# Masked softmax with per-batch lengths: the load of batch 3 is cut in halves that go behind the first two stores, and GpSimd's start is rearranged

## Chip, cores, metric

One core of a Trainium2 chip. The metric is the device time of one execution in microseconds; medians of several executions are given.

## The reference

For each of 16 batches there are 8 heads of 256 x 256 float32. Only the first `length` columns of a row count; the others come out as zero.

```python
for b in range(batch):
    length = lengths[b]                      # 128..255, known only at run time
    masked = x[b, :, :, :length]
    e = np.exp(masked - masked.max(-1, keepdims=True))
    result[b, :, :, :length] = e / e.sum(-1, keepdims=True)   # the rest stays 0
```

## The kernel before

A batch is one slot of a tile with 8 slots: 128 partitions x 16 rows x 256 columns, 2 MB. SyncE loads batches 0 to 3 whole (0 in halves). GpSimd loads 4 to 15, each only as wide as its length needs, into slots whose right part it has filled with zeros. Per batch VectorE masks (`clip`), ScalarE takes the exponential and the row sums, VectorE divides in two halves, and SyncE stores (most batches as a half and two quarters).

```python
        for h in range(2):                                  # load 0 in halves
            s = slice(h * half, (h + 1) * half)
            nc.sync.dma_start(out=xt[:, 0, s], in_=x_f[0, :, s]).then_inc(s_ld[h], 16)
        nc.scalar.dma_start(out=word64, in_=lengths[None, :]).then_inc(s_word, 16)
        for b in range(1, ahead):                           # loads 1, 2, 3; ahead = 4
            nc.sync.dma_start(out=xt[:, b], in_=x_f[b]).then_inc(s_ld[b + 1], 16)
        for b in range(batch):                              # all stores, same queue
            s_b = s_st[b % 2]
            for s in parts(b):
                nc.sync.wait_ge(s_out, 2 * b + (s.stop - 1) // half + 1)
                ...
                nc.sync.dma_start(out=out_f[b, :, s, :], in_=xt[:, b % slots, s, :]
                ).then_inc(s_b, 16 * ((s.stop - s.start) // quarter))
        ...
        # GpSimd
        nc.gpsimd.dma_start(out=word64_p, in_=lengths[None, :]).then_inc(s_word_p, 16)
        ...
        nc.gpsimd.wait_ge(s_v, 1)                           # VectorE's first step
        for b in range(ahead, slots):
            nc.gpsimd.memset(xt[:, b, :, low:], 0.0).then_inc(s_fill, 1)
        nc.gpsimd.wait_ge(s_word_p, 16)
        nc.gpsimd.wait_ge(s_fill, slots - ahead)
        nc.gpsimd.wait_ge(s_ld[ahead - 1], 16)              # load 2 has landed
        # ... then the loads of batches 4 to 15, two in flight
        ...
        # VectorE, start: cast of the lengths, matmul broadcasts them, bounds in step 2
        nc.vector.wait_ge(s_word, 16)
        nc.vector.tensor_copy(out=len_b, in_=word[:, ::2]).then_inc(s_lenb, 1)
        nc.vector.wait_ge(s_lenf, 1)
        step(nc.vector.tensor_scalar(out=len_s, in0=len_f, scalar1=big, ...))   # s_v = 2
```

VectorE's order is mask 0a, mask 0b, divide 0a, mask 1, divide 0b, mask 2, divide 1a, divide 1b, mask 3, and so on (a and b are the halves of a batch). A store waits for its divide. At most two batches of stores are in flight.

The softmax here doesn't subtract the row's maximum and nothing guards it: scores larger than these inputs give would overflow.

## Time and profile before

| | before |
|---|---|
| median time | 157.06 us (3 runs, 156.97 to 157.08) |
| bytes moved | 62.08 MB |
| busiest compute engine | VectorE, 77% |
| both DMA queues, share of the 16 engines' time | 65.9% + 32.0% |
| first store: issued, first packet | 16.73 us, 23.43 us |
| first load of GpSimd: issued, first packet | 20.71 us, 25.71 us |

The last two rows join the timeline with the packet records. The page's DMA row gives the busy tenths of the DMA engines in 40 slices of 3.9 us, and the row below it GB/s. A high digit with low GB/s means that packets are in flight but slow. The lines themselves stand in the prediction.

### The profile page before, as it was taken

The page shows a single profiled execution, that of the slowest core. Times are in us where ns is not written, and L with a number is a line of the kernel's source. Part 1 is how long each engine was busy: PE and PEld are TensorE (multiplying, and loading weights), DVE is VectorE, ACT ScalarE, POOL GpSimd, SP SyncE. Part 2 cuts the span into 40 slices and gives each one's busy share as a digit, 9 for nine tenths or more (in the row PEclk, how much of TensorE's full clock was granted, in tenths as well). Part 3 has the DMA queues.
Part 4 walks back from the last instruction along what each step waited for, and adds up shares of the span by engine and source line. Part 5 has one row for each costly group of instructions (what it writes and reads, how often), then busy time and mean ns, then how long its engine had stood idle before and what let it go on. Part 6 is the DMA issues. An engine that isn't in the chain of part 4 may idle for free.

```text
span 155.5 us, 1320 instructions
## 1 busy us (share of the span) xinstructions
PE 0.2 (0%) x1; PEld 0.1 (0%) x1; DVE 120.0 (77%) x84; ACT 105.1 (68%) x514; POOL 19.4 (12%) x26
## 2 busy tenths in 40 slices
PE   0000000000000000000000000000000000000000
PEld 0000000000000000000000000000000000000000
DVE  4963999999999968939895999997977999920000
ACT  3029599999989893956969298989592989400000
POOL 7900031003020202002020202020100000000000
DMA  4999999999999999999999999999999999999991
GB/s 116 428 443 426 434 312 388 416 442 427 393 395 410 415 416 406 420 410 413 409 412 419 402 417 406 415 411 405 425 421 432 420 419 432 457 426 422 415 434 61
DMA packets 10452, 62.08 MB, mean 399 GB/s; under 512 B 930, under 2 KB 1026, under 8 KB 7122
## 3 DMA queue, kind: packets, MB, share of 16 engines
q1 hardware_dynamic: 6336, 41.95, 65.9%
q0 software_dynamic: 4112, 20.12, 32.0%
q14 instruction: 2, 0.02, 0.0%
q10 hardware_dynamic: 2, 0.00, 0.0%
HBM read 28.51 MB, written 33.55 MB: 399 GB/s over the span
## 4 chain that ended last, share of the span: by engine, by line
DMA 67%; DVE 11%; issue 6%; POOLq 2%; SPq 1%; POOL 0%; DVEq 0%
DMA xt<-in_x_dram 60%; DVE xt L224 7%; DMA out_dram<-xt 7%; DVE xt L197 3%; POOLq L100 1%; POOLq L136 1%; POOLq L131 1%; SPq L109 1%; DVE inv_sum L221 0%; POOL xt L131 0%; SPq L112 0%; POOLq L159 0%; POOLq L155 0%; DVEq L214 0%; POOLq L161 0%
## 5 line engine op out<-in xcount | busy, mean ns | idle before, releaser
L251 ACT ACTIVATE xt<-xt x256 | 102.4, 402 | 27.2 <-DVE xt L197 27.2
L224 DVE TENSOR_TENSOR xt<-xt,inv_sum 128x2048 f32<-128x2048 f32 x32 | 73.3, 2292 | 1.1
L251 ACT ACTIVATION_READ_ACCUMULATOR xt<-xt x256 | 48.2, 188 | 0.0
L197 DVE SCALAR_TENSOR_TENSOR xt<-down,len_s,xt 128x2048 f32<-128x2048 f32 (+1 forms) x17 | 37.7, 2222 | 11.1 <-DMA xt<-in_x_dram 10.2
L131 POOL DMA_DIRECT2D xt<-in_x_dram x12 | 12.7, 1057 | 89.7 <-issue 45.7
L221 DVE RECIPROCAL inv_sum<-row_sum 128x8 f32<-128x8 f32 x32 | 6.2, 195 | 2.4 <-ACT xt L251 2.4
L185 DVE CAST len_b<-word 1x16 bf16<-1x16 int32 x1 | 5.6, 5595 | 0.4 <-DMA word<-in_lengths_dram 0.4
L151 POOL MEMSET xt<- 128x1536 f32 x4 | 5.3, 1392 | 0.0
L243 ACT ACT_TABLE_LOAD x1 | 1.3, 1283 | 1.6 <-SPq L79 1.6
L180 DVE TENSOR_SCALAR down<-iota_i 128x256 f32<-128x256 int32 x1 | 0.3, 295 | 1.6 <-POOL iota_i L142 1.6
L146 POOL DMA_DIRECT2D word_p<-in_lengths_dram x1 | 0.6, 643 | 0.1
L188 DVE TENSOR_SCALAR len_s<-len_f 128x16 f32<-128x16 f32 x1 | 0.2, 174 | 0.4 <-PE len_f L167 0.4
L142 POOL IOTA iota_i<- 128x256 int32 x1 | 0.3, 331 | 0.6 <-SPq L79 0.6
L243 ACT ACTIVATE warm<-const-float32-0.0 128x1 f32<-128x1 f32 x1 | 0.2, 203 | 0.0
L145 POOL MEMSET ones<- 1x128 bf16 x1 | 0.2, 194 | 0.0
L167 PE MATMUL len_f<-len_b,ones 1*128 1x16 bf16 x1 | 0.2, 168 | 8.0 <-DVE len_b L185 8.0
L269 POOL MEMSET const-float32-0.0<- 128x1 f32 x1 | 0.1, 98 | 0.3 <-issue 0.3
L148 POOL MEMSET seed<- 1x1 f32 x2 | 0.1, 88 | 0.0
L167 PEld LDWEIGHTS len_f<-len_b,ones 1*128 1x128 bf16 x1 | 0.1, 98 | 8.0 <-issue 8.0
L269 POOL MEMSET const-float32-1.0<- 128x1 f32 x1 | 0.1, 98 | 0.0
L269 POOL MEMSET const-bfloat16-1.0<- 128x1 bf16 x1 | 0.1, 98 | 0.0
L269 POOL MEMSET const-uint8-127<- 128x1 uint8 x1 | 0.1, 98 | 0.0
(1 smaller groups left out, 0.0 us busy)
## 6 DMA issues: line engine op xcount, KB each, us to landing
out_dram<-xt SPq DMA_DIRECT2D x16, 1024.0 KB
out_dram<-xt SPq DMA_DIRECT2D x20, 512.0 KB
xt<-in_x_dram SPq DMA_DIRECT2D x3, 2048.0 KB, 16.0
out_dram<-xt SPq DMA_DIRECT2D x3, 2048.0 KB
xt<-in_x_dram POOLq DMA_DIRECT2D x3, 1728.0 KB, 15.9
xt<-in_x_dram POOLq DMA_DIRECT2D x2, 2048.0 KB, 16.0
xt<-in_x_dram POOLq DMA_DIRECT2D x2, 1600.0 KB, 14.5
xt<-in_x_dram POOLq DMA_DIRECT2D x2, 1280.0 KB, 13.6
```

What stands on the lines that cost most here:

```text
L100: return nc.values_load(at, engines=[engine], skip_runtime_bounds_check_because="compared with constants, never an address",)
L109: nc.sync.dma_start(out=xt[:, 0, s], in_=x_f[0, :, s]).then_inc(s_ld[h], 16)
L131: nc.gpsimd.dma_start(out=xt[:, slot, :, :w], in_=x_n[:, n, :, :w]).then_inc(s_sw[par], 16)
L136: with nc.gpsimd.If(v <= ws[m]):
L146: nc.gpsimd.dma_start(out=word64_p, in_=lengths[None, :]).then_inc(s_word_p, 16)
L151: nc.gpsimd.memset(xt[:, b, :, low:], 0.0).then_inc(s_fill, 1)
L185: nc.vector.tensor_copy(out=len_b, in_=word[:, ::2]).then_inc(s_lenb, 1)
L197: return nc.vector.scalar_tensor_tensor(out=t, in0=down[:, None, lo:hi].to_broadcast([P, s.stop - s.start, hi - lo]), scalar=len_s[:, b : ...
L221: step(nc.vector.reciprocal(out=inv_sum[:, b, s], in_=row_sum[:, b, s]))
L224: nc.vector.tensor_tensor(out=t, in0=t, in1=inv_sum[:, b, s, None].to_broadcast([P, half, seq_k]), op=ALU.mult,).then_inc(s_out, 1)
L243: nc.scalar.activation(out=warm, in_=nc.const_aps.tensor(0.0, (P, 1), F32), func=EXP)
L251: ins = nc.scalar.activation(out=e, in_=e, func=EXP, accum_out=sum_h[:, bass.ds(i, 1), j])
```

## The change

Two ideas. First, SyncE issues load 3 in halves, one behind store 0a and one behind store 0b, so that the first store need not queue behind all of load 3; store 0b then goes out in one piece instead of two quarters. Second, the fills wait for the bounds (the scaled lengths in every partition, VectorE's second step), so that they don't hold up VectorE's cast of the lengths, and GpSimd reads the lengths that ScalarE fetched.

```diff
         def parts(b):
-        if b < 10:
+        if b == 0:
+            cuts = [0, half, nt]
+        elif b < 10:
             cuts = [0, half, half + quarter, nt]
 ...
-        for b in range(1, ahead):
+        for b in range(1, ahead - 1):
             nc.sync.dma_start(out=xt[:, b], in_=x_f[b]).then_inc(s_ld[b + 1], 16)
+        last = [
+            (s_ld[ahead + h], slice(h * half, (h + 1) * half)) for h in range(2)
+        ]
 ...                                        # behind each store, while halves are left:
+                if last:
+                    s_l, r = last.pop(0)
+                    nc.sync.dma_start(out=xt[:, ahead - 1, r], in_=x_f[ahead - 1, :, r]).then_inc(s_l, 16)
 ...
-        nc.gpsimd.dma_start(out=word64_p, in_=lengths[None, :]).then_inc(s_word_p, 16)
 ...
-        nc.gpsimd.wait_ge(s_v, 1)
+        nc.gpsimd.wait_ge(s_v, 2)
 ...
-        nc.gpsimd.wait_ge(s_word_p, 16)
+        nc.gpsimd.wait_ge(s_word, 16)
 ...                                        # VectorE, mask of batch 3:
+                if b == ahead - 1:
+                    nc.vector.wait_ge(s_ld[b + 2], 16)
```

More of the change, by code (lines that the diff above doesn't have):

```diff
@@ L65 @@
     word = word64.bitcast(I32)
-    word64_p = pool.tile([1, batch], mybir.dt.int64, name="word64_p")
-    word_p = word64_p.bitcast(I32)
     len_b = pool.tile([1, batch], BF16, name="len_b")
@@ L81 @@
         s_word = sem("s_word")
-        s_word_p = sem("s_word_p")
         s_ones = sem("s_ones")
@@ L85 @@
         s_lenf = sem("s_lenf")
-        s_ld = [sem(f"s_ld{k}") for k in range(ahead + 1)]
+        s_ld = [sem(f"s_ld{k}") for k in range(ahead + 2)]
         s_sw = [sem("s_sw0"), sem("s_sw1")]
@@ L104, in length @@
             )
+        nc.scalar.dma_start(out=word64, in_=lengths[None, :]).then_inc(s_word, 16)
         for h in range(2):
@@ L109 @@
             nc.sync.dma_start(out=xt[:, 0, s], in_=x_f[0, :, s]).then_inc(s_ld[h], 16)
-        nc.scalar.dma_start(out=word64, in_=lengths[None, :]).then_inc(s_word, 16)
-        for b in range(1, ahead):
+        for b in range(1, ahead - 1):
             nc.sync.dma_start(out=xt[:, b], in_=x_f[b]).then_inc(s_ld[b + 1], 16)
+        last = [
+            (s_ld[ahead + h], slice(h * half, (h + 1) * half)) for h in range(2)
+        ]
         for b in range(batch):
@@ L157 @@
                 n = 2 * q + (ahead + par)
-                v_len = length(POOL, word_p[0:1, bass.ds(2 * n, 1)])
+                v_len = length(POOL, word[0:1, bass.ds(2 * n, 1)])
                 with nc.gpsimd.If(q >= 1):
```

## The prediction

> **What bounds the kernel now.** I read the page first: engines, slices, queues.
>
> ```profile
> PE 0.2 (0%) x1; PEld 0.1 (0%) x1; DVE 120.0 (77%) x84; ACT 105.1 (68%) x514; POOL 19.4 (12%) x26
> ...
> DMA  4999999999999999999999999999999999999991
> GB/s 116 428 443 426 434 312 388 416 442 427 393 395 410 415 416 406 420 410 413 409 412 419 402 417 406 415 411 405 425 421 432 420 419 432 457 426 422 415 434 61
> ...
> q1 hardware_dynamic: 6336, 41.95, 65.9%
> q0 software_dynamic: 4112, 20.12, 32.0%
> ```
>
> No compute engine is above 77%, while the DMA row is at 9 from the second slice to the last but one. SyncE's queue (q1) and GpSimd's (q0) fill 97.9% of the 16 engines' time. So the bound is bytes through the DMA engines: 62.08 MB. A change can win only where the engines move less than they could. One slice stands out, the sixth with 312. I cut the span finer (columns: stretch, length, busy time of each engine, clock, DMA share, GB/s):
>
> ```profile
> 2.00:3.00 1.00, 0.00 (x0) 0.00 (x0) 0.70 (x1) 0.99 (x2) 1.00 (x4) 1.00 0.93 205
> 3.00:4.00 1.00, 0.00 (x0) 0.00 (x0) 1.00 (x1) 0.14 (x1) 1.00 (x2) 1.00 0.82 287
> ...
> 8.00:20.00 12.00, 0.17 (x1) 0.10 (x1) 8.42 (x8) 7.28 (x36) 0.00 (x0) 1.00 1.01 432
> 20.00:21.00 1.00, 0.00 (x0) 0.00 (x0) 1.00 (x1) 1.00 (x7) 0.28 (x1) 1.00 1.34 426
> 21.00:22.00 1.00, 0.00 (x0) 0.00 (x0) 1.00 (x2) 1.00 (x6) 0.92 (x1) 1.00 1.19 279
> 22.00:23.00 1.00, 0.00 (x0) 0.00 (x0) 1.00 (x1) 1.00 (x7) 0.00 (x0) 1.00 0.57 197
> 23.00:24.00 1.00, 0.00 (x0) 0.00 (x0) 0.97 (x3) 1.00 (x6) 0.51 (x1) 1.00 0.73 270
> 24.00:25.00 1.00, 0.00 (x0) 0.00 (x0) 1.00 (x1) 1.00 (x7) 0.03 (x1) 1.00 0.96 393
> ...
> 41.00:123.00 82.00, 0.00 (x0) 0.00 (x0) 71.09 (x51) 64.99 (x321) 9.77 (x9) 1.00 1.02 413
> 123.00:152.00 29.00, 0.00 (x0) 0.00 (x0) 13.85 (x10) 10.34 (x52) 0.00 (x0) 1.00 1.01 428
> ```
>
> 432 GB/s is what a stretch of whole loads reaches; I take it as the rate to lose against. From 20 to 25 us the loss is 6+153+235+162+39 = 595 KB, or 1.4 us at 432. From the first packet (2.14 us in the packet records) to 4 us some 492 KB moved where 804 could: 0.7 us. From 41 to 123 us 413 stands against 432, 3.6 us in all, but there the software queue moves packets of 1.3 to 4.8 KB, and the change leaves those alone. After the last load (123.7 us) stores alone still run for 30 us at 428: VectorE ends at 137, the last packet at 153.5. Compute has 16 us of slack at the end.
>
> The chain of waits then tells where GpSimd's loads start, and the timeline what VectorE does at the start:
>
> ```profile
> 2.51 16.01 DMA xt<-in_x_dram
> 18.52 0.02 issue
> ```
> ```profile
> 1.83 0.64 POOL L146 DMA_DIRECT2D word_p<-in_lengths_dram  x1
> 2.04 1.90 SPq L112 DMA_DIRECT2D xt<-in_x_dram  x3
> 2.30 5.59 DVE L185 CAST len_b<-word 1x16 bf16<-1x16 int32 x1 [0.40 <-DMA word<-in_lengths_dram]
> 2.47 0.12 POOL L148 MEMSET seed<- 1x1 f32 x2
> 2.54 5.33 POOL L151 MEMSET xt<- 128x1536 f32 x4
> ```
>
> The third whole load (batch 2) lands at 18.52 and opens GpSimd's gate. A cast of 16 numbers takes 5.59 us and ends (7.89) when the four fills do (7.87). Behind it come the matmul, the bounds, and the first mask at 9.29.
>
> **What the Trainium skill says.** "SBUF — State Buffer", section Who interferes with whom: a cast may run in a mode that takes the port pair shared with GpSimd, and then one of the two blocks fully; a VectorE instruction with two SBUF inputs meets GpSimd only where GpSimd reads. The cast agrees (both end within 0.02 us); that the mask (two inputs) runs freely beside a fill (which only writes) no trace here shows yet. "DMA: Bandwidth & Descriptors", section Queues, rings and completion order: an engine alternates between the queues that have work, packet by packet. The packet records agree: from 26 to 32 us q1 moves about 190 GB/s and q0 about 230. Same page, Issuing engines are not separate DMA queues: which engine starts a transfer changes no bandwidth. The 432 of q1 alone against 413 of both agrees that a second queue adds nothing. Same page, Specifications: first byte of the software path about 1 us. The trace disagrees: GpSimd's first x load is issued at 20.71 and its first packet starts at 25.71, and the lengths take 1.83 to about 6.0.
>
> **The change part by part.**
>
> *Fills after the bounds.* The cast starts at 2.30 with no fill running; I give it 0.1 us (estimate: other small VectorE steps took 0.17 to 0.2). Matmul and bounds took 8.01 to 8.42 after the cast, so the bounds stand at about 2.9. The first mask then waits for the first half load, which lands at 6.2 (issue 1.13 plus 5.1, the shorter of the two half loads). Mask from 9.29 to about 6.4: 2.9 us earlier. The second half lands at 8.7, and ScalarE reaches it later. From first mask to first store took 9.29 to 16.73 = 7.44 us, so the first store goes out at 13.8, the second half's at 21.4 - 2.9 = 18.5. The fills move to about 3.0 to 8.4, long before the gate at 18.5. None of these 2.9 us is on the path that sets the end: they only make stores ready.
>
> *Removed lengths load on GpSimd.* 0.64 us of issue and some 4-byte packets. It may have disturbed the first packets (some took 1.0 us instead of 0.31 just after it); at best the 0.7 us of the start. I count 0.2.
>
> *Halves of batch 3 between the stores.* Before, q1 held load 3 from 18.0 to 23.9 and the first store's packets began at 23.4, 6.7 us after issue. Now at 18.0 (end of load 2's packets) q1 finds store 0a, issued at 13.8. At 1.05 MB each and 432 GB/s, 2.43 us: store 0a 18.0 to 20.4, half load 3a to 22.9, store 0b (issued at 18.5, in time) to 25.3, then half load 3b. q0 starts at about 25.7 as before, since its gate is load 2. By then q1 has moved the same bytes in both kernels, only in another order. Load 3b has about 0.9 MB left, which at q1's shared 200 GB/s takes 4.4 us: it lands near 30.5 instead of 24.25. VectorE wants it at 28.46 - 2.9 = 25.6, so a new wait of about 5 us appears in front of the mask of batch 3, and that mask runs some 2 us later than before. Meanwhile q1 has both halves of store 1 (issued at 23.3 and 25.7; 2.1 MB, 10 us at 200 GB/s) and q0 two loads, so the engines do not run dry. No bytes are saved.
>
> Sum: the DMA time stays, except the two weak spots. The start gives 0.2. The 1.4 us at 20 to 25 us: I do not know its cause. Direction changes alone are not it, for at 34 to 38 us loads and stores alternate at 430 GB/s. It begins with GpSimd's first large issue (20.71), which stays; but later issues, as at 36.24, show no dip. I give 35% that it vanishes (-0.5), 50% that it stays, 15% that the three changes of direction in q1 add about 1.3 us (+0.2). 157.06 - 0.2 - 0.5 + 0.2 = 156.6; I say 156.5.
>
> **The rivals.**
>
> *A new wait takes over:* the mask of batch 3 waits for its second half and the delay reaches the end. For: VectorE is in order, and its mask of batch 4 and GpSimd's slots lie behind it. Against: VectorE needs 7.1 us per batch (2.35 + 2 x 2.45) while the DMA delivers one per 9.3 us (3.88 MB at 415), so 2 us are caught up within one or two batches; at the end 16 us are spare. If the queues did run dry for the 2 us: 159.
>
> *The early start is worth its full size:* stores begin 5.4 us sooner and the end moves with them. For: the first store's packets wait 6.7 us behind a load. Against: the engines were busy with that load, which must be done anyway. It would make 152 to 154.
>
> *The dip is load into store within one queue:* now there are two such turns and one back. For: the dip lies exactly on load 3's last three packets per engine (0.65 to 1.38 us instead of 0.61) and ends as the first store packet starts. Against: the mixed stretch without loss. It would make 158 to 158.5.
>
> *The dip goes altogether, and the start is clean:* 155.0.
>
> **Range and chances.** The sure part is zero, the weak spots allow -2.1 and the turns +1.4, with run-to-run spread 0.1. I take 155.3 to 157.7. Faster than 2% needs 153.9, below what both weak spots give; slower than 2% needs 160.2, beyond the dry-queue case. 0.02 and 0.02.
>
> **What would show each step right or wrong.** The cast well under 1 us, the first mask near 6.4 beside the fills at its usual 1.24 us; first store issued near 13.8. Load 3b landing near 30 and a VectorE wait before batch 3's mask. GpSimd's first load still issued near 20.7. In the fine stretches: whether 20 to 25 us stays near 300 GB/s, and the first 2 us. I am wrong if the DMA row falls below 9 between 25 and 45 us (queues dry), if GpSimd's first load comes later because it is now its first transfer, or if the 41 to 123 us rate moves away from 413.

## The result

The changed kernel takes 157.01 us (4 runs, 156.81 to 157.34), the kernel before 157.01 us (4 runs, 156.94 to 157.08). The ratio is 1.0002, 95% interval 0.9984 to 1.002: the same.

The page of the changed kernel, its engines, slices and queues:

```profile
PE 0.2 (0%) x1; PEld 0.1 (0%) x1; DVE 115.2 (74%) x84; ACT 105.3 (68%) x514; POOL 19.0 (12%) x25
...
DMA  4999999999999999999999999999999999999992
GB/s 110 425 438 432 322 423 421 411 411 443 414 404 389 418 406 420 411 408 421 406 416 412 410 421 403 414 409 411 416 409 438 425 423 427 444 432 436 423 413 121
...
q1 hardware_dynamic: 6336, 41.95, 66.1%
q0 software_dynamic: 4080, 20.12, 32.1%
```

The DMA row is as full as before and the bytes are the same. The weak slice has not gone: it was the sixth (312), now it is the fifth (322). The fine stretches of the changed kernel, with columns as in the prediction:

```profile
2.00:3.00 1.00, 0.17 (x1) 0.10 (x1) 0.34 (x2) 0.99 (x2) 0.00 (x0) 1.00 1.02 197
3.00:4.00 1.00, 0.00 (x0) 0.00 (x0) 0.00 (x0) 0.14 (x1) 0.95 (x1) 1.00 0.88 270
9.00:15.00 6.00, 0.00 (x0) 0.00 (x0) 4.82 (x4) 5.56 (x28) 0.00 (x0) 1.00 1.01 431
15.00:16.00 1.00, 0.00 (x0) 0.00 (x0) 1.00 (x1) 0.00 (x0) 0.00 (x0) 1.00 1.21 459
16.00:17.00 1.00, 0.00 (x0) 0.00 (x0) 0.97 (x3) 0.52 (x3) 0.00 (x0) 1.00 1.28 328
17.00:18.00 1.00, 0.00 (x0) 0.00 (x0) 1.00 (x1) 1.00 (x5) 0.00 (x0) 1.00 0.74 246
18.00:19.00 1.00, 0.00 (x0) 0.00 (x0) 0.67 (x1) 1.00 (x7) 0.00 (x0) 1.00 0.62 254
19.00:20.00 1.00, 0.00 (x0) 0.00 (x0) 0.36 (x1) 1.00 (x6) 0.00 (x0) 1.00 1.02 434
20.00:25.00 5.00, 0.00 (x0) 0.00 (x0) 4.93 (x5) 5.00 (x27) 1.59 (x2) 1.00 1.01 423
...
41.00:123.00 82.00, 0.00 (x0) 0.00 (x0) 70.94 (x49) 64.94 (x320) 9.75 (x9) 1.00 1.02 412
123.00:152.00 29.00, 0.00 (x0) 0.00 (x0) 17.09 (x14) 12.99 (x64) 0.00 (x0) 1.00 1.00 427
```

The stretch of slow packets lies from 16 to 19 us, some 5 us earlier than before, and ends where the packets of store 0a begin (18.33 us in the packet records, 23.43 before). By then GpSimd has issued no load at all. From 20 to 25 us, where before was at its worst, the rate is 423. The start (197, 270) is no better than before (205, 287), and the long mixed part is unchanged (412 against 413).

The chain of waits and the timeline of the changed kernel:

```profile
2.51 16.89 DMA xt<-in_x_dram
19.40 0.02 issue
```
```profile
2.30 0.17 DVE L189 CAST len_b<-word 1x16 bf16<-1x16 int32 x1 [0.39 <-DMA word<-in_lengths_dram]
...
3.05 5.33 POOL L155 MEMSET xt<- 128x1536 f32 x4 [1.11 <-DVE len_s L192]
6.51 1.28 DVE L201 SCALAR_TENSOR_TENSOR xt<-down,len_s,xt 128x1024 f32<-128x1024 f32 x1 [3.52 <-DMA xt<-in_x_dram]
...
13.95 0.42 SPq L121 DMA_DIRECT2D out_dram<-xt  x1
14.41 0.36 SPq L126 DMA_DIRECT2D xt<-in_x_dram  x1
...
31.28 2.35 DVE L201 SCALAR_TENSOR_TENSOR xt<-down,len_s,xt 128x2048 f32<-128x2048 f32 x1 [4.41 <-DMA xt<-in_x_dram]
```

The cast takes 0.17 us instead of 5.59. The first mask starts at 6.51 and takes its 1.28 us in the middle of the fills. The first store goes out at 13.95 instead of 16.73. Load 2 is the one that the slow stretch now hits: it lands at 19.40 instead of 18.52, and GpSimd's first load is issued 1.07 us later than before (21.78). The mask of batch 3 waits 4.41 us for the second half of its load. VectorE's gain of 2.9 us at the start has turned into a loss of 2.8 us there (31.28 against 28.46), and still the time is the same.

So two questions are left. What is the slow stretch, and does it cost what it seems? And why does a VectorE that is first earlier and then later not matter: is the whole change idle, or do two effects cancel?

### The profile page after: what moved, and what is told of

Its sections match the earlier page's. It is cut to its first block, busy times and chain, and to the rows that moved or that the text cites. A ratio compares the mean times of both kernels' runs of the same rounds, so it can differ in the third digit from the quotient of the medians.

```text
span 154.9 us, 1320 instructions
## 1 busy us (share of the span) xinstructions
PE 0.2 (0%) x1; PEld 0.1 (0%) x1; DVE 115.2 (74%) x84; ACT 105.3 (68%) x514; POOL 19.0 (12%) x25
## 4 chain that ended last, share of the span: by engine, by line
DMA 71%; DVE 12%; issue 3%; SPq 3%; POOLq 1%; DVEq 0%
DMA out_dram<-xt 40%; DMA xt<-in_x_dram 31%; DVE xt L230 9%; DVE xt L201 3%; SPq L121 2%; SPq L109 1%; DVE inv_sum L227 0%; POOLq L99 0%; SPq L111 0%; POOLq L136 0%; POOLq L141 0%; POOLq L159 0%; DVEq L220 0%; POOLq L163 0%; SPq L120 0%
## 5 line engine op out<-in xcount | busy, mean ns | idle before, releaser
L189 DVE CAST len_b<-word 1x16 bf16<-1x16 int32 x1 | 0.2, 165 | 0.4 <-DMA word<-in_lengths_dram 0.4
```

## The experiments

The theories as the runs were planned. **D:** the DMA engines set the time, so neither part of the change matters. Its rival: the parts have effects that cancel. For the slow stretch, **F:** it is paid once, for the first store of the program; **T:** it is a turn from 16 KB load packets to stores in SyncE's queue; **G:** GpSimd's first large issue causes it (the trace of the changed kernel already speaks against G, since the stretch comes 5 us before that issue). A table of all readings of the slow stretch stands after the runs. The kernel before took a median of 156.91 us beside the first four runs, 156.93 beside the next four, then 156.97 and 157.14.

### fills_only: the second part alone

```diff
 # the kernel before, with:
-        nc.gpsimd.dma_start(out=word64_p, in_=lengths[None, :]).then_inc(s_word_p, 16)
-        nc.gpsimd.wait_ge(s_v, 1)
+        nc.gpsimd.wait_ge(s_v, 2)
-        nc.gpsimd.wait_ge(s_word_p, 16)
+        nc.gpsimd.wait_ge(s_word, 16)
```

> The kernel before with the second part of the change alone (shared lengths, fills after the bounds). My theory (the DMA engines set the time, and an earlier store only waits longer in SyncE's queue): the first store is issued near 13.9 us instead of 16.7, its packets still begin near 23.4 behind load 3, the weak stretch stays at 20 to 24 us (near 280, 200, 270 GB/s), ratio to before 0.998 to 1.002. Rival (the earlier compute start is worth something by itself): ratio below 0.995.

Measured: 157.09 us (6 runs), ratio 1.0012, interval 0.9989 to 1.0036. The first mask is at 6.41 us and the first store is issued at 13.85, as meant. In the fine stretches the weak seconds are where they were in the kernel before:

```profile
21.00:22.00 1.00, 0.00 (x0) 0.00 (x0) 0.96 (x3) 1.00 (x7) 0.98 (x1) 1.00 1.09 246
22.00:23.00 1.00, 0.00 (x0) 0.00 (x0) 1.00 (x1) 1.00 (x6) 0.00 (x0) 1.00 0.63 213
23.00:24.00 1.00, 0.00 (x0) 0.00 (x0) 0.97 (x3) 1.00 (x7) 0.50 (x1) 1.00 0.71 270
```

With the old order an earlier start is worth nothing: the store waits 2.9 us longer behind load 3. It also shows that the slow stretch doesn't follow the time at which the store is issued (13.85 against 16.73); it follows the place of the store in the queue.

### order_only: the first part alone

```diff
 # the changed kernel, with the second part undone:
+        nc.gpsimd.dma_start(out=word64_p, in_=lengths[None, :]).then_inc(s_word_p, 16)
-        nc.gpsimd.wait_ge(s_v, 2)
+        nc.gpsimd.wait_ge(s_v, 1)
-        nc.gpsimd.wait_ge(s_word, 16)
+        nc.gpsimd.wait_ge(s_word_p, 16)
```

> The changed kernel with the second part undone (GpSimd's own lengths load, fills before the bounds). My theory: cast 5.6 us and first store near 16.7 us as before, still ahead of the end of load 2's packets at 18 us, so the queue has no gap; the weak stretch lies at 16 to 18.5 us, before the first store's packets; ratio 0.997 to 1.003. Rival (the order needs the earlier store, else the queue runs dry between load 2 and store 0): ratio above 1.005.

Measured: 158.71 us (6 runs, 158.26 to 159.02), ratio 1.0106, interval 1.008 to 1.0132. My theory missed: the order alone costs some 1.7 us. (This run undoes both halves of the second part, the place of the fills and GpSimd's own load of the lengths; no run tells the two apart.) The reason that the rival gave is not what the trace shows either; store 0a was issued at 16.74, in time for the end of load 2. The loss is elsewhere, and the fine stretches of this kernel and its timeline show it:

```profile
28.00:31.00 3.00, 0.00 (x0) 0.00 (x0) 0.55 (x1) 3.00 (x17) 0.00 (x0) 1.00 0.99 300
31.00:41.00 10.00, 0.00 (x0) 0.00 (x0) 5.93 (x5) 4.50 (x23) 0.49 (x1) 1.00 1.03 431
```
```profile
35.01 2.35 DVE L205 SCALAR_TENSOR_TENSOR xt<-down,len_s,xt 128x2048 f32<-128x2048 f32 x1 [6.45 <-DMA xt<-in_x_dram]
```

From 28 to 31 us the rate is 300 where the changed kernel has 413 in the same stretch: 3 us x (413 - 300) / 432 = 0.8 us lost. The packet records show both queues at loads then (the second half of load 3, and batch 4), with slow packets in both. The engines also drift apart: the second half of load 3 lands on its first engine at 29.1 us and on its last at 34.7 (changed kernel: 29.0 and 31.0). At the very end the last half store lands on fourteen engines by 153.9 us and on the last two at 155.3 and 155.4, where the changed kernel is done at 153.3. So about half of the loss is a slower stretch and the rest two engines that fell behind, by the account of this one profile. It isn't a queue run dry: VectorE is 3.7 us later than in the changed kernel at the mask of batch 3 (35.01 against 31.28), but afterwards the rate is as high (431 from 31 to 41 us against 429, 403 from 41 to 48 us against 399). Why the packets are slow from 28 to 31 us is open. Two kernels below have a weaker dip there (halves_all 369, act_big 376).

### after_warm and before_warm: a tiny early store on ScalarE's queue

```diff
 # the changed kernel, or the kernel before, with:
         nc.scalar.dma_start(out=word64, in_=lengths[None, :]).then_inc(s_word, 16)
+        nc.vector.memset(zero, 0.0).then_inc(s_zero, 1)          # [128, 128] float32
+        nc.scalar.wait_ge(s_zero, 1)
+        nc.scalar.dma_start(out=out_f[0, :, 0, 0:P], in_=zero).then_inc(s_warm, 16)
 ...
+        nc.sync.wait_ge(s_warm, 16)                               # before the first real store
```

> The changed kernel with one tiny early store (128 rows of 512 B of zeros, overwritten later) from ScalarE's queue at about 1.7 us. Theory F (the weak stretch of some 1.2 us is paid once, for the first store of the program, wherever it comes): the stretch at 16 to 18.5 us is gone (above 420 GB/s), time lower by 0.7 to 1.3 us unless it is paid at the start instead, which would show as a worse 2 to 4 us. Theory T (it is the turn from 16 KB load packets to store packets within SyncE's queue): the stretch at 16 to 18.5 us stays near 320, 240, 370 GB/s and the ratio is 1.000 within 0.003.

> The same tiny early store in the kernel before. Theory F: 20 to 24 us rises from 426, 279, 197, 270 to above 400 each, time lower by 0.7 to 1.3 us. Theory T: unchanged there, ratio 1.000 within 0.003. A third (GpSimd's first large issue at 20.7 us does it): unchanged here too, but it has to explain why the changed kernel has the stretch 4 us before that issue.

Measured: after_warm 157.05 us, ratio 1.0004 (0.9982 to 1.0026); before_warm 156.94 us, ratio 1.0007 (0.9981 to 1.0032). The slow stretch stays in both. These 64 KB touch only 512 B of every 8 KB that store 0a writes, so they don't show whether the stretch comes from writing that part of the output for the first time; early_store below does. This looked like T, and it was wrong to read it so, as the next runs show.

### halves_all and whole_between: which packets lie ahead of the store

```diff
 # halves_all: the changed kernel, with
         for b in range(1, ahead - 1):
-            nc.sync.dma_start(out=xt[:, b], in_=x_f[b]).then_inc(s_ld[b + 1], 16)
+            for h in range(2):
+                s = slice(h * half, (h + 1) * half)
+                nc.sync.dma_start(out=xt[:, b, s], in_=x_f[b, :, s]).then_inc(s_ld[b + 1], 16)
 # (waits for loads 1 and 2 raised to 32)
 # whole_between: the changed kernel, with
-        last = [(s_ld[ahead + h], slice(h * half, (h + 1) * half)) for h in range(2)]
+        last = [(s_ld[ahead], slice(0, nt))]          # load 3 whole, behind store 0a
```

> The changed kernel with loads 1 and 2 as halves too, so that the packets ahead of the first store are 8 KB like the store's and not 16 KB. If the weak stretch hangs on the 16 KB load packets, it is gone at 16 to 18.5 us (above 400 GB/s) and the ratio to before is about 0.993. If it belongs to the first store of SyncE's queue whatever the packets, it stays (about 1.2 us lost) and the ratio is 0.998 to 1.003.

> The changed kernel with load 3 whole (16 KB packets) between store 0a and store 0b. If every turn from 16 KB loads to stores costs, there is a second weak stretch near 24 to 26 us, 1.2 us lost more, ratio 1.005 to 1.008. If only the first store costs, no second stretch and 0.998 to 1.003; the landing of load 3 then moves to about 27 us, ahead of 30.97.

Measured: halves_all 156.82 us, ratio 0.9992 (0.9965 to 1.0018); whole_between 157.16 us, ratio 1.0003 (0.9975 to 1.0031). With 8 KB packets ahead the stretch stays. With a second turn from 16 KB loads to stores no second stretch appears (410 GB/s from 22 to 28 us), and load 3 lands at 27.2 us. T falls: neither the size of the load packets ahead of the store nor a later turn matters.

### early_store, tiny_sp, act_big: a store of another size, on another queue, earlier

```diff
 # the changed kernel; zero is [128, 4, 256] float32 = 512 KB, in tiny_sp [128, 128] = 64 KB
 # early_store and tiny_sp, between loads 0 and 1 on SyncE's queue:
+        nc.vector.memset(zero, 0.0).then_inc(s_zero, 1)
+        nc.sync.wait_ge(s_zero, 1)
+        nc.sync.dma_start(out=out_f[batch - 1, :, 0:4, :], in_=zero).then_inc(s_warm, 16)
 # act_big: the same 512 KB with nc.scalar, right behind the lengths
 # all: nc.sync.wait_ge(s_warm, 16) before the first real store
```

> The changed kernel with a 512 KB store of zeros on SyncE's own queue between loads 0 and 1 (512 KB more bytes, 1.2 us at 432 GB/s, overwritten later). If the loss is paid once by the first full-size store of SyncE's queue, it shows near 6 to 9 us and the stretch before store 0a, now near 17 to 20 us, is clean: ratio about 1.008. If the loss belongs to the turn before store 0a whatever went earlier, it stays there, and the ratio is about 1.008 with one stretch or 1.015 with two.

> The changed kernel with a 64 KB store of zeros (128 rows of 512 B) on SyncE's own queue between loads 0 and 1. If what is paid once belongs to the queue that stores for the first time, 15 to 20 us is clean (loss at 432 GB/s below 0.2 us instead of 0.88), and about 1 us is lost near 6 to 9 us instead, or less if a small store pays less; ratio between 0.994 and 1.002. If it belongs to the amount (only a store of some size pays it), 15 to 20 us keeps its 0.9 to 1.1 us and the ratio is 1.001.

> The changed kernel with a 512 KB store of zeros on ScalarE's queue, issued near 1.7 us (1.2 us more of bytes). If the amount decides, SyncE's first store is clean afterwards (15 to 20 us loses below 0.2 us). If the queue decides, the 0.9 to 1.1 us stay there, whatever ScalarE's queue lost before.

Measured: early_store 158.67 us, ratio 1.0108 (1.0076 to 1.014); tiny_sp 156.93 us, ratio 0.9998 (0.9966 to 1.003); act_big 157.66 us, ratio 1.0042 (1.0003 to 1.0081). The fine stretches of early_store:

```profile
5.00:10.00 5.00, 0.00 (x0) 0.00 (x0) 1.51 (x2) 1.87 (x9) 3.45 (x3) 1.00 1.05 372
...
15.00:25.00 10.00, 0.00 (x0) 0.00 (x0) 8.27 (x6) 5.83 (x29) 1.29 (x1) 1.00 1.00 423
```

and of tiny_sp:

```profile
5.00:10.00 5.00, 0.00 (x0) 0.00 (x0) 2.42 (x2) 2.05 (x11) 3.37 (x3) 1.00 1.06 442
...
15.00:25.00 10.00, 0.00 (x0) 0.00 (x0) 8.89 (x8) 8.48 (x43) 1.68 (x2) 1.00 0.99 378
```

and of act_big:

```profile
5.00:10.00 5.00, 0.00 (x0) 0.00 (x0) 1.28 (x1) 1.80 (x9) 3.46 (x3) 1.00 1.05 411
...
15.00:25.00 10.00, 0.00 (x0) 0.00 (x0) 9.43 (x7) 7.21 (x37) 1.30 (x1) 1.00 1.00 418
```

A 512 KB store moves the slow stretch to itself, and store 0a is then clean. Its zeros go to batch 15, so the part of the output that store 0a writes is still untouched: first use of that memory isn't the cause. A 64 KB store in the same place of the same queue doesn't do it. act_big shows that it need not be SyncE's queue: 512 KB on ScalarE's leave SyncE's first store clean as well (418). So F holds with a condition: the stretch comes with the first store that is large enough. Where the limit lies isn't settled: 64 KB were too little in three kernels, but in sp_first below they cut the loss from 1.2 to 0.7 us, and the 64 KB also went in packets of 512 B against 4 KB, so amount and packet size aren't told apart. Both kernels pay for it with bytes, 0.524 MB / 432 GB/s = 1.2 us or 0.77% of the time, so neither ratio alone says much on the size of the loss. In act_big it looks smaller (411 GB/s from 5 to 10 us against 439: 5 us x 28 / 432 = 0.3 us), and with the same added bytes act_big is 1.0 us faster than early_store. So it isn't shown that the loss has one size wherever it falls, which is why first_on_act below was tried.

### sp_first and first_on_act: can the loss be dodged?

```diff
 # sp_first: the changed kernel with tiny_sp's 64 KB store ahead of the loads on SyncE's queue
 # first_on_act: the changed kernel; SyncE skips store 0a, and ScalarE, behind its first
 # two groups of exponentials, does
+        nc.scalar.wait_ge(s_out, 1)
+        nc.scalar.dma_start(out=out_f[0, :, :half, :], in_=xt[:, 0, :half, :]).then_inc(
+            s_st[0], 16 * (half // quarter)
+        )
```

> The changed kernel with the 64 KB store of zeros as the very first transfer of SyncE's queue, before the loads; a try at a faster kernel. If the queue's first store pays, and pays while the engines have little to do yet, 15 to 20 us is clean and the start loses less than the 0.9 us saved: ratio 0.994 to 0.998. If the loss is the same wherever it falls, ratio 1.000 to 1.003, with the loads landing some 0.5 to 1 us later. If a small store does not pay it, 15 to 20 us keeps its loss and the ratio is about 1.003.

> A try at a faster kernel: the changed kernel with store 0a alone on ScalarE's queue, so that the program's first large store runs packet by packet beside load 2 on SyncE's queue and not behind it. The run with 512 KB of zeros on ScalarE's queue lost about 0.4 us (at 432 GB/s) where the changed kernel loses 0.88 us at 15 to 20 us; if that carries over, 14 to 21 us loses 0.3 to 0.6 us and the ratio is 0.995 to 0.999. Against it: load 2 lands some 2 us later (near 21 us), and with it GpSimd's first load; if that matters the ratio is 1.000 to 1.006. If the loss is the same on any queue, the ratio is 1.000 to 1.003.

Measured: sp_first 157.43 us, ratio 1.0034 (1.0005 to 1.0063): the start falls to 111 GB/s from 2 to 4 us, and 15 to 25 us recovers in part only (401: 10 us x (432 - 401) / 432 = 0.7 us lost there instead of 1.2). first_on_act 156.96 us, ratio 0.9988 (0.996 to 1.0016): the stretch stays at 16 to 19 us; ScalarE's store, issued at 13.95 us, shows its first packet at 18.06 us only, near the end of the stretch, so the store that was to run beside load 2 did so for its last 1.5 us alone (to 19.52). Neither beats the two kernels clearly.

All readings of the slow stretch, in GB/s from the same fine stretches:

| kernel | 5 to 10 us | 15 to 25 us | ratio to before |
|---|---|---|---|
| before | 436 | 374 | 1 |
| changed | 439 | 383 | 1.0002 |
| fills_only | 444 | 372 | 1.0012 |
| order_only | 444 | 374 | 1.0106 |
| before_warm | 433 | 374 | 1.0007 |
| after_warm | 431 | 380 | 1.0004 |
| halves_all | 428 | 383 | 0.9992 |
| whole_between | 437 | 385 | 1.0003 |
| tiny_sp | 442 | 378 | 0.9998 |
| first_on_act | 433 | 380 | 0.9988 |
| sp_first | 437 | 401 | 1.0034 |
| act_big | 411 | 418 | 1.0042 |
| early_store | 372 | 423 | 1.0108 |
| late_3b (below) | 441 | 371 | 1.0089 |

371 to 385 in eleven of the fourteen is one and the same loss, 10 us x (432 - 380) / 432 = 1.2 us at their middle, wherever in those 10 us it lies. A packet is counted whole in one second or another here, so single seconds are coarse.

### late_3b: how late may VectorE be?

```diff
 # the changed kernel: the second half of load 3 goes behind store 1a, not 0b
-                if last:
+                if last and s.start == 0:
```

> The changed kernel with the second half of load 3 behind store 1a instead of 0b, so that VectorE's wait for it (4.4 us) grows by about 4 to 8 us. If a later VectorE is hidden behind the DMA engines (my argument), the ratio stays 0.998 to 1.004. If the room is used up by then, SyncE's queue runs dry of stores, the rate falls below 400 GB/s somewhere from 30 to 45 us, and the ratio is above 1.01, as in the run with the order alone (1.0106).

Measured: 158.29 us (6 runs), ratio 1.0089, interval 1.0055 to 1.0122. VectorE waits 12.0 us for load 3 and starts that mask at 39.05 us instead of 31.28. The fine stretches of this kernel show what it costs:

```profile
31.00:42.00 11.00, 0.00 (x0) 0.00 (x0) 2.92 (x3) 0.35 (x2) 1.16 (x1) 1.00 1.01 416
42.00:48.00 6.00, 0.00 (x0) 0.00 (x0) 5.97 (x4) 6.00 (x32) 1.15 (x1) 1.00 1.04 318
```

Until 42 us the engines live on what is queued. Then SyncE's queue is dry (2 to 29 GB/s of its own from 43 to 47 us in the packet records): the first store of batch 2 is issued at 43.87 us only, and its first packet starts at 46.91. 6 us x (432 - 318) / 432 = 1.6 us are lost. So the room that VectorE has in the changed kernel is real but short: a wait of 4.4 us costs nothing that the time shows, one of 12 us does.

## Why the prediction was right or wrong

The class, the range and the direction of the two big arguments held; the point (156.5 against 157.01) was 0.5 us low. There was luck in it: each part was priced by itself at about nothing, and the order alone, so priced, measures +1.7 us.

- *Bound.* Right. The queues fill 98.2% of the engines' time, the bytes are the same, the mixed part keeps its rate, and the time is the same.
- *Fills after the bounds.* The sizes held: cast 0.17 us (0.1 predicted), first mask 6.51 (6.4), stores 0a and 0b at 13.95 and 18.70 (13.8, 18.5). "None of these 2.9 us is on the path that sets the end" is half right. fills_only shows it for the old order. With the new order the second part as a whole is worth 1%: without it order_only takes 1.0106. What I left out is that the two parts act on each other. How is not shown: late_3b shows that VectorE's room can be used up, but order_only lost its time with no queue dry, so that the earlier start pays for room that the new order spends is a guess, and GpSimd's lengths load is untested. Neither part alone gains. (The mask's "usual 1.24 us" was half of a merged line of two overlapping masks; one takes 1.28 to 1.29.)
- *Removed lengths load.* The 0.2 us are not there: 2 to 4 us carries 233 GB/s in the changed kernel, 246 before.
- *Halves between the stores.* The order of packets came as worked out, with the second half landing at 30.97 (30.5) and a wait of 4.4 us (5). GpSimd's first load slipped to 21.78, which I had at 20.7, because the slow stretch now sits in the load that opens its gate.
- *The weak stretch.* This is the step that failed. "It begins with GpSimd's first large issue (20.71), which stays" named a coincidence. The stretch moved some 5 us ahead, to the first store, while that issue came later. The rival about load into store in one queue had the place right and the count wrong: the later turn that whole_between adds is free, so the stretch comes once in both kernels, and the 15% for a loss of 1.3 us were as idle as the 35% for a gain. The 50% for "it stays" came true in size, not in place. Shown: the loss goes to the first large store. Not shown: what in the chip is slow then. It can't be the store's own packets alone, as the loads ahead of it are the slow ones in the changed kernel (16 KB packets of up to 1.26 us instead of 0.61); in order_only, where no load was left ahead, the store's own were (8 KB packets at a median of 0.60 us from 20 to 21 us instead of 0.31).
- *The rivals.* "A new wait takes over" was named with 159 for a queue that runs dry; late_3b is that case, at 158.29. In its argument the sum was wrong (2.35 + 2 x 2.45 is 7.25 us per batch, not 7.1), which changes nothing against the 9.3 us of the DMA. "The early start is worth its full size" (152 to 154) is excluded by fills_only and by the result.

## What to carry to other kernels

Where transfers bind, as here, an earlier start of the compute engines can be worth nothing (fills_only), and a later one can be hidden until a queue runs dry (late_3b); so ask how many microseconds of queued transfers stand between a late engine and a dry queue, and test it by making it later. When a change has two parts, run each alone: a result of "no difference" can be two parts that need each other. A slow stretch beside a striking event is not caused by it until the event has been moved and the stretch has moved along.

## What the Trainium skill lacked or had wrong

- No page has the loss at the first large store: around the first store of 1 MB about 1.2 us are lost to packets at about half speed, once in each of these kernels. Behind an early store of 512 KB, on SyncE's or ScalarE's queue, it is gone (15 to 25 us: 423 and 418 GB/s); behind 64 KB it isn't (374 to 380), save in part where they came before all loads (401).
- "DMA: Bandwidth & Descriptors", Specifications: a first byte after about 1 us on GpSimd's path. Here GpSimd's first x load needs 5.0 us from issue to first packet (20.71 to 25.71), in the changed kernel 5.4 us (21.78 to 27.18). The path is not the reason: beside SyncE's busy queue ScalarE's stores took as long (after_warm 1.67 to 5.70, act_big 2.36 to 6.55, first_on_act 13.95 to 18.06), while SyncE's very first load, with nothing else in flight, took 1.0 us (1.13 to 2.14). So 1 us is not refuted for GpSimd with idle engines, which no run has; what is lacking is the wait of 4 to 5 us for a queue that joins a busy one.
- "DMA: Bandwidth & Descriptors", Anatomy of one DMA: a fixed cost of about 2 us, most of it the receipt of the write after the last byte. That section is about GpSimd's path; there the last load lands 0.7 us after its last packet in the kernel before (123.00 to 123.66). On SyncE's here, load 3 lands 0.3 us after its last packet (23.96 to 24.25 us) and the last store 0.5 us after its own (153.47 to 153.94). Whether a packet's record already holds the receipt isn't shown.
- "SBUF — State Buffer", Who interferes with whom, was neither lacking nor wrong: the mask, with two SBUF inputs, takes 1.28 us beside a GpSimd fill and 1.29 us without one, as that section has it.
